# A transformer block on one core: modulation columns on the matrix engine, four load buffers, and another rank for row products

## The chip, the cores and the metric

The kernel runs on one core of one Trainium2 chip. The core has a matrix engine (TensorE, PE in the profile, with PEld for its weight loads), VectorE (DVE), ScalarE (ACT), GpSimd (POOL) and SyncE (SP), which here only issues loads. Matmuls write to PSUM, everything else lies in SBUF, and DMA engines move data between the chip's memory (HBM) and SBUF. Each engine works through its own queue in order and waits on semaphores for the others.

The metric is the device time of one execution in microseconds (us).

## The reference

The block has 256 tokens of width 2048, all in float32. What matters here is its beginning: a conditioning vector c gives a modulation vector of 12288 numbers, and its first third shifts and scales the normed input, which then meets the wide projection.

```
mod = jnp.einsum('bd,de->be', jax.nn.silu(c), w_ada[l]) + b_ada[l]
sh1, sc1, gt1, sh2, sc2, gt2 = jnp.split(mod[:, None, :], 6, axis=-1)
h = rms_norm(x, norm1_g[l]) * (1.0 + sc1) + sh1
proj = jnp.einsum('btd,dc->btc', h, w_in[l])
...
x = x + gt1 * (mixed @ w_out[l])
h = rms_norm(x, norm2_g[l]) * (1.0 + sc2) + sh2
x = x + gt2 * (jnp.square(jax.nn.relu(h @ w_up[l])) @ w_down[l])
```

`w_ada` is 2048 x 12288 and `w_in` 2048 x 10064. Between the projection and `w_out` lie a recurrent part and an attention part, which the change doesn't touch.

## The kernel before

**Layout and split matmuls.** Activations lie transposed: features on the 128 partitions in 16 chunks, tokens along the rows. A float32 product is built from three faster products: each operand is split into a rounded high part and the rest (`hhi` and `hlo` for the input, `whi` and `wlo` for weights). `split` (L190) does this for weights: ScalarE casts the loaded piece `wr` to `whi` (L193), VectorE subtracts to get `wlo` (L90).

**Modulation columns.** The number of a column of 128 modulation values is e: e = j is the shift of chunk j, e = 16 + j its scale. `ada_long(e)` (L165) loads 128 rows of the transposed `w_ada` (2048 long, 1 MB) into a slot of the tiles `ap0` and `ap1`, and `ada_dot` (L156) lets VectorE multiply them with a row `sb`, which holds silu(c) times two on every partition, and sum along the row: one *row product* gives one column of `modc`. Four slots are used for the first four loads, then two in turn (L167). A load waits until the product that read its slot is done.

**Rounds.** The projection's sum over the 16 chunks is cut into rounds: chunks 0-1, 2-3, 4-7, 8-11, 12-15 (L182). A round begins with `modulate` (L326), for each chunk: VectorE scales the normed input (`hf`), ScalarE adds the shift and rounds it (`hhi`), VectorE forms `hlo`. Its factor `am` (L387) is taken for all chunks of a round at once, so it needs all scale columns of the round. Then nine groups of output columns follow (L394): for each pair of chunks a weight piece is loaded (`weights`, L221, four buffers `wr`), split, and used in 24 matmuls (18 in the first group, which is narrower). Seven groups are evicted after each round: copied by ScalarE in the first, added to their tile by VectorE (L361) in later ones. The two groups `pvp` stay in four PSUM banks through all rounds.

The columns that a round needs are loaded in the round before: `next_ada` (L236) is called after each weight piece and takes e from the list `later` at the rate `pace`. The four columns for the first round are loaded at the start.

**Order.** The program is written with priorities: `START` comes before `STREAM` (weight loads, splits, evictions and row products), and this before `MAIN` (matmuls and the rest). A planner works out a timeline from its own estimates, takes for each engine what is ready with the best priority, and so fixes each engine's order at build time. `tc.issue_after(i)` makes an instruction come after i; `hold` and `ahold` are lists from which row products and splits take such a predecessor. After the rounds, other projections and later modulation columns are mixed into the recurrent and attention parts.

**PSUM.** Tiles named with `PX` take four banks in turn; among them are `pss` (sums of squares for the first norm) and the four `pvp`.

Of the kernel before, what the change touches and what calls it, by code (L numbers as in the profile page):

```python
# [17 lines left out]
T = 256  # L18
# [5 lines left out]


P_BADA, P_N1, P_N2, P_MU, P_A0, P_KK, P_KA, P_RK, P_LNW, P_LNB = 0, 96, 112, 128, 155, 163, 171, 179, 187, 195
P_QG, P_KG0, P_KG1, P_KG2, P_PEK, P_PEV, NPRM = 203, 204, 205, 206, 207, 223, 239

C_ID, C_MSK, C_HS, C_ONE, C_BLK, C_CUM, C_SEL, NCST = 0, 128, 192, 224, 225, 353, 609, 737

# [2 lines left out]
def block_kernel(ctx, tc, a):  # L33
# [58 lines left out]
    def stt(out, x, s, y, op0, op1):  # L92
        return V.scalar_tensor_tensor(out, x, s, y, op0=op0, op1=op1).ins  # L93
# [12 lines left out]
    STREAM = 0  # L106
    MAIN = 1 << 20
    START = -(1 << 20)


    tc.cur_priority = START
# [44 lines left out]
    def ada_dot(r, s, start, out):  # L156
        with behind():
            V.tensor_tensor_reduce(out=r, in0=r, in1=s, scale=0.5, scalar=start,  # L158
                                    op0=OP.mult, op1=OP.add, accum_out=out)

    apb = [B16("ap0", [128, 2, D]), B16("ap1", [128, 2, D])]
    apn = [0]
    SLOTS = 2

    def ada_long(e):  # L165

        n = apn[0] if apn[0] < 4 else apn[0] % SLOTS  # L167
        r = apb[n // 2][:, n % 2]
        apn[0] += 1
        nc.sync.dma_start(r, a["w_ada_t"][e * 128:(e + 1) * 128])  # L170
        ada_dot(r, sb, prm[:, P_BADA + e:P_BADA + e + 1], modc[:, e:e + 1])

    def ada(e):

# [5 lines left out]
                    modc[:, e:e + 1] if h else part)  # L180

    rounds = [(0, 2), (2, 2), (4, 4), (8, 4), (12, 4)]  # L182
    for j in range(rounds[0][1]):
        ada_long(j)
        ada_long(16 + j)


    ahold = []
# [54 lines left out]
    def proj(segs_of, W, ms, rhi, rlo, kps, evac, banks=None, first=True, last=True):  # L243


        nb = (len(ms) + 1) // 2
        ps = banks or [PM("pp") for _ in range(nb)]
        for i, kp in enumerate(kps):
            hi, lo = weights(segs_of(kp), W)
            next_ada(ada_long if starting[0] else ada)  # L250
            todo = [[(k, m) for m in range(len(ms))] for k in range(2)]
            if 0 and i == len(kps) - 1 and nb == 2:
                todo = [[(k, m) for k in range(2) for m in range(len(ms)) if m // 2 == b] for b in range(2)]
            for part in todo:
                for k, m in part:
                    (c0, cw), kc = ms[m], 2 * kp + k
                    o = ps[m // 2][0:cw, (m % 2) * 256:(m % 2) * 256 + 256]
                    mm3(o, hi[:, k, c0:c0 + cw], lo[:, k, c0:c0 + cw], rhi[:, kc], rlo[:, kc],
                        first and i == 0 and k == 0 and m % 2 == 0, last and i == len(kps) - 1 and k == 1)
                yield  # L260
        if evac:
            with prio(STREAM):
                for b in range(nb):
                    evac(b, ps[b])
# [24 lines left out]
        act(sq, xn[:, 2 * i:2 * i + 2], AF.Square)  # L289
        tt(sqs, sqs, sq, OP.add)  # L290
    for k in range(2):
        mm(pss, ones, sqs[:, k], k == 0, k == 1)

    def log_exp(behind):

# [5 lines left out]
    def rsqrt(out, x, scale, ep, tmp):  # L301

        e0 = {0.0: 0, 1e-6: 1, 64e-5: 2}[ep]
        act(out, x, AF.Ln, scale=scale, bias=eps[0:x.shape[0], e0:e0 + 1])
        i = act(out, out, AF.Exp, scale=-0.5)
        tt(tmp, out, out, OP.mult)
        stt(tmp, x, ep / scale, tmp, OP.add, OP.mult)
        stt(tmp, tmp, -0.5 * scale, out, OP.mult, OP.mult)
        stt(out, out, 1.5, tmp, OP.mult, OP.add)
        return i  # L310

    rs = T2("rs", [128, T])
    with tc.issue_after(log_exp([lastt])):
        rsqrt(rs, pss, 1.0 / D, 1e-6, T2("rst", [128, T]))

    hhi = B16("hhi", [128, KC, T], FR)
    hlo = B16("hlo", [128, KC, T], FR)
# [30 lines left out]
    pq = B8("pq", [128, 8, T])  # L348
    spq = dr.tile([128, 8, T], FT, name="spq")
    pl = cst.tile([128, 3, T], FT, name="pl")  # L350
    pvp = [PX("pvp") for _ in range(4)]
    M4 = [(i * 128, 128) for i in range(4)]

    def acc_evac(dst, first, last):
# [15 lines left out]
        groups.append(([(i * 512, 512)], 512, M4,  # L370
                       lambda b, i=i: (prk[:, i // 2, (i % 2) * 4 + 2 * b:(i % 2) * 4 + 2 * b + 2], 128, None), None))
    for i in range(2):
        groups.append(([(2048 + i * 512, 512)], 512, M4, None, pvp[2 * i:2 * i + 2]))
    for i in range(2):
        groups.append(([(i * 512, 512)], 512, M4,
                       lambda b, i=i: (prk[:, i // 2, (i % 2) * 4 + 2 * b:(i % 2) * 4 + 2 * b + 2], 128, None), None))
# [7 lines left out]
    for r, (j0, n) in enumerate(rounds):  # L384
        first, last = r == 0, r == len(rounds) - 1
        with prio(START + (1 << 18)):
            stt(am[:, j0:j0 + n], modc[:, 16 + j0:16 + j0 + n], 1.0, prm[:, P_N1 + j0:P_N1 + j0 + n], OP.add, OP.mult)  # L387
            lasth = modulate(j0, n, xn)
            if first:
                hold.extend([lasth] * 0 + [None])  # L390
        if not last:
            later.extend(e for j in range(j0 + n, sum(rounds[r + 1])) for e in (j, 16 + j))
            pace[:] = [len(later) / (len(groups) * n // 2 - 1), 0]
        for cols, W, ms, dst, banks in groups:  # L394
            g = proj(wseg(cols), W, ms, hhi, hlo, range(j0 // 2, (j0 + n) // 2),
                     dst and acc_evac(dst, first, last), banks, first or banks is None, last or banks is None)
            if last and dst and cols[0][0] >= 3360 and W == 512:
                queue.append(g)
            else:
                run(g)  # L400
        assert not later
# [731 lines left out]
            lastss[0] = mm(ps[:, 0:T], ones, x[:, i], k == 0 and i == 0, k == 1 and i == 1)  # L1133
    rs2 = T2("rs2", [128, T])
    with tc.issue_after(le):
        i = rsqrt(rs2, ps[:, 0:T], 1.0 / D, 1e-6, T2("rst2", [128, T]))
    ahold[:0] = [i, i]
    for q, t in ((0, 0), (0, 1), (1, 0)):
        tokens(q, t)
# [113 lines left out]
def _pack(inp):  # L1253

    g = {k: v[0] if k != "rel_bias" else v for k, v in inp.items()}
    p = np.zeros((128, NPRM), np.float32)

    def cols(at, v):
        v = v.reshape(-1, 128)
        p[:, at:at + v.shape[0]] = v.T  # L1260

    cols(P_BADA, g["b_ada"])
    cols(P_N1, g["norm1_g"])
    cols(P_N2, g["norm2_g"])
    cols(P_MU, g["rwkv_mu"][:3328])
    p[64:96, P_MU + 26] = g["rwkv_mu"][3328:]
    for at, k in ((P_A0, "rwkv_a0"), (P_KK, "rwkv_k_k"), (P_KA, "rwkv_k_a"), (P_LNW, "rwkv_ln_w"), (P_LNB, "rwkv_ln_b")):
        cols(at, g[k])
    cols(P_RK, g["rwkv_r_k"].reshape(-1))
    for at, v in ((P_QG, g["q_norm_g"]), (P_KG0, g["k_norm_g"][0]), (P_KG1, g["k_norm_g"][1]), (P_KG2, g["k_norm_g"][2])):  # L1270
        p[:, at] = np.concatenate([v, v])
    for at, k in ((P_PEK, "cmp_pe_k"), (P_PEV, "cmp_pe_v")):
        p[:, at:at + 16] = g[k].reshape(16, 2, 64).transpose(1, 2, 0).reshape(128, 16)
    c, onehot = _consts()
    out = {
        "xT": g["x"].T, "c": g["c"], "w_ada_t": g["w_ada"].T, "w_in": g["w_in"], "params": p, "consts": c,
        "onehot": onehot, "w2a": np.concatenate([g["rwkv_w2"], g["rwkv_w0"][None]]), "a2": g["rwkv_a2"],
        "g2": g["rwkv_g2"], "w1k": g["cmp_w1_k"], "w2k": g["cmp_w2_k"], "w1v": g["cmp_w1_v"], "w2v": g["cmp_w2_v"],
        "rel_bias": g["rel_bias"], "w_o_rwkv": g["w_o_rwkv"], "w_o_nsa": g["w_o_nsa"], "w_out": g["w_out"],
        "w_up": g["w_up"], "w_down": g["w_down"],  # L1280
    }
    return {k: np.ascontiguousarray(v) for k, v in out.items()}
# [17 lines left out]
```

## Time and profile before

| | us |
|---|---|
| median of 3 runs | 1642.96 |
| runs | 1642.14 to 1643.19 |
| the profiled execution | 1648.3 |
| its span, first to last instruction | 1646.5 |
| first matmul of round 0 starts | 27.89 |
| last row product of the rounds starts | 176.0 |

All later views are of the profiled execution, and times in them count from the start of its span. In a row of the timeline stand start, duration, engine, line, operation, output <- inputs with shapes, and in brackets how long the engine was idle before it and for whom it waited. In a row of groups the count is followed by busy us in total, mean ns of one, and the idle time before them. Helpers share lines: all matmuls are L99, most VectorE operations L90 and L93, so the names of the tiles tell them apart. In a row of waits stand who waited, for whom, the us in total, the number of waits and the longest. A few per cent of the matmul records are missing from the trace.

### The profile page before, as it was taken

How to read it: one execution, taken by the hardware profiler on the slowest of the kernel's cores; microseconds unless marked ns; L12 is line 12 of the kernel's file. 1: busy time of each engine (PE TensorE's matmuls, PEld its weight loads, DVE VectorE, ACT ScalarE, POOL GpSimd, SP SyncE). 2: the span in 40 equal slices, each digit the busy share in tenths (PEclk: the TensorE clock that was granted, in tenths of full speed). 3: DMA queues.
4: the chain of work that ended last, by engine and by line, in shares of the span. 5: the costliest groups of instructions: out<-in, count | busy, mean ns of one | idle time of the engine just before them, and what ended most of it. 6: DMA issues, size and time to landing. Idle time of an engine off the chain costs nothing.

```text
span 1646.5 us, 28130 instructions
## 1 busy us (share of the span) xinstructions
PE 1564.2 (95%) x11291; PEld 1380.2 (84%) x11291; DVE 1149.4 (70%) x1695; ACT 756.3 (46%) x1112; POOL 34.9 (2%) x60
## 2 busy tenths in 40 slices
PE   5969999999999889999999899999999999999998
PEld 4968998878889879777899788888888888888886
DVE  7999876977788766777876776666655555555555
ACT  4423358526423365656534444444444544444442
POOL 0000000000000000000000000000000000000001
PEclk9989999998999999999999999999999999999999
DMA  9999767673988777655687477878776555555564
GB/s 371 319 325 342 247 183 236 215 200 120 324 245 276 251 262 258 237 180 167 212 287 269 153 242 239 264 244 260 242 217 189 204 194 193 192 192 194 194 194 148
DMA packets 171174, 381.99 MB, mean 232 GB/s; under 512 B 29249, under 2 KB 43905, under 8 KB 166690
## 3 DMA queue, kind: packets, MB, share of 16 engines
q1 hardware_dynamic: 149344, 355.79, 65.6%
q0 software_dynamic: 4176, 14.17, 2.4%
q10 hardware_dynamic: 17523, 10.24, 2.2%
q8 instruction: 88, 1.44, 0.3%
q14 instruction: 43, 0.35, 0.1%
HBM read 370.13 MB, written 10.01 MB: 231 GB/s over the span
## 4 chain that ended last, share of the span: by engine, by line
PE 48%; DMA 4%; DVE 3%; issue 1%; ACT 1%; DVEq 0%; ACTq 0%
PE pu L99 21%; PE da L99 10%; PE db L99 10%; PE pp L99 5%; DMA ar<-in_w_ada_t 2%; DMA wr<-in_w_out 1%; DVE wlo L90 1%; PE po L99 1%; PE sps L99 1%; DMA gate<-sma 0%; ACT whi L193 0%; PE ptp L1012 0%; DVE ar L158 0%; DVE o L90 0%; ACT p L87 0%
## 5 line engine op out<-in xcount | busy, mean ns | idle before, releaser
L193 ACT CAST whi<-wr 128x1024 fp32r<-128x1024 f32 (+1 forms) x352 | 367.0, 1043 | 513.4 <-PE pp L99 125.6
L90 DVE TENSOR_TENSOR wlo<-wr,whi 128x1024 fp32r<-128x1024 f32 (+1 forms) x352 | 425.8, 1213 | 171.8 <-ACT whi L193 168.7
L99 PE MATMUL pp<-hhi,whi 128*128 128x256 f32 (+1 forms) x1072 | 309.9, 293 | 25.1 <-ACT hhi L87 22.5
L99 PE MATMUL pp<-hlo,whi 128*128 128x256 f32 (+1 forms) x1072 | 307.4, 289 | 0.2 <-DVE hlo L93 0.2
L99 PE MATMUL pp<-hhi,wlo 128*128 128x256 f32 (+1 forms) x1072 | 301.2, 290 | 6.6 <-DVE wlo L90 6.6
L90 DVE TENSOR_TENSOR wdl<-wd,wdh 128x1024 fp32r<-128x1024 f32 x128 | 156.6, 1225 | 170.9 <-ACT wdh L193 170.9
L99 PEld LDWEIGHTS pp<-hhi,whi 128*128 128x128 f32 (+1 forms) x1072 | 209.9, 197 | 33.8 <-ACT hhi L87 23.4
L193 ACT CAST wdh<-wd 128x1024 fp32r<-128x1024 f32 x128 | 134.9, 1055 | 193.7 <-PE db L99 188.6
L99 PEld LDWEIGHTS pp<-hhi,wlo 128*128 128x128 f32 (+1 forms) x1072 | 205.5, 196 | 13.0 <-DVE wlo L90 8.5
L99 PEld LDWEIGHTS pp<-hlo,whi 128*128 128x128 f32 (+1 forms) x1072 | 210.5, 196 | 5.0 <-issue 3.7
L99 PE MATMUL pu<-h2a,whi 128*128 128x512 f32 x512 | 177.2, 398 | 3.1 <-DVE h2a L93 3.1
L99 PE MATMUL pu<-h2b,whi 128*128 128x512 f32 x512 | 179.1, 397 | 0.8 <-DVE h2b L93 0.8
L99 PE MATMUL pu<-h2b,wlo 128*128 128x256 f32 x512 | 140.9, 280 | 0.0
L99 PE MATMUL pu<-h2a,wlo 128*128 128x256 f32 x512 | 135.9, 281 | 0.0
L158 DVE CUSTOM_DVE_ANT_0 ar<-ar,sb,prm 128x1024 f32<-128x1024 f32 x64 | 82.1, 1282 | 73.0 <-DMA ar<-in_w_ada_t 72.9
L99 PEld LDWEIGHTS pu<-h2b,whi 128*128 128x128 f32 x512 | 95.8, 188 | 23.9 <-DVE h2b L93 1.2
L99 PEld LDWEIGHTS pu<-h2a,whi 128*128 128x128 f32 x512 | 95.2, 189 | 24.4 <-DVE h2a L93 3.4
L99 PEld LDWEIGHTS pu<-h2a,wlo 128*128 128x128 f32 x512 | 95.5, 190 | 2.2
L158 DVE CUSTOM_DVE_ANT_0 ar<-ar,sb,adap 128x1024 f32<-128x1024 f32 x64 | 82.0, 1281 | 21.2 <-DMA ar<-in_w_ada_t 20.9
L99 PEld LDWEIGHTS pu<-h2b,wlo 128*128 128x128 f32 x512 | 95.9, 189 | 0.5
L99 PE MATMUL db<-wdh,ul 128*128 128x512 f32 x256 | 79.6, 389 | 0.0
L99 PE MATMUL db<-wdl,uh 128*128 128x512 f32 x256 | 79.6, 389 | 0.0
(342 smaller groups left out, 2676.6 us busy)
## 6 DMA issues: line engine op xcount, KB each, us to landing
wr<-in_w_in SPq DMA_DIRECT2D x136, 512.0 KB, 5.1
ar<-in_w_ada_t SPq DMA_DIRECT2D x128, 512.0 KB, 4.8
wr<-in_w_up SPq DMA_DIRECT2D x128, 512.0 KB, 4.3
wd<-in_w_down SPq DMA_DIRECT2D x128, 512.0 KB, 4.3
ap<-in_w_ada_t SPq DMA_DIRECT2D x32, 1024.0 KB, 6.6
wr<-in_w_out SPq DMA_DIRECT2D x32, 512.0 KB, 5.4
wr<-in_w_in SPq DMA_DIRECT2D x40, 256.0 KB, 3.4
wr<-in_w_o_rwkv SPq DMA_DIRECT2D x16, 512.0 KB, 4.9
```

Source lines behind the costliest of these rows:

```text
L90: return V.tensor_tensor(out, x, y, op=op).ins
L99: return PE.matmul(out, l, r, start=start, stop=stop, skip_group_check=True).ins
L158: V.tensor_tensor_reduce(out=r, in0=r, in1=s, scale=0.5, scalar=start, op0=OP.mult, op1=OP.add, accum_out=out)
L193: S.copy(hi, raw)
```

## The change

Six things change in the first rounds.

1. The columns of chunks 0 to 3 (e = 0-3 and 16-19) are no longer row products. `ada_pair` makes four columns at a time on TensorE: for j = 0 (e = 0, 1, 16, 17) and j = 2. The host lays out `w_ada` a second time for them (`w_ada_p`), in 1 MB pieces of 128 x 2048; `scz` holds silu(c) times two by chunk in the first of 32 columns and zeros in the others. Each of four loads gives four matmuls into the four 32-row strips of one PSUM bank, with the load as moving operand. ScalarE copies the bank, four matmuls with a column of ones sum the strips, and VectorE adds the bias.
2. The load slots are four throughout, not two after the first four.
3. In round 0 the list `later` holds the four loads of pair j = 2 and the columns 4, 20 and 5 of the third round, at a rate of 0.9 per weight piece; round 1 loads the remaining five at 5/8.
4. Row products get the priority `DOTS`, after `STREAM` and before `MAIN`.
5. In round 0 the `pvp` groups come last, since the two pairs use the same four PSUM banks before them.
6. In the start, the first three casts come after the first norm's exponential, the first `wlo` after the norm's last operation and the next two after the round's modulation.

```diff
+    DOTS = 1 << 19
...
-    SLOTS = 2
...
-        n = apn[0] if apn[0] < 4 else apn[0] % SLOTS
+        n = apn[0] % 4
         r = apb[n // 2][:, n % 2]
         apn[0] += 1
         nc.sync.dma_start(r, a["w_ada_t"][e * 128:(e + 1) * 128])
-        ada_dot(r, sb, prm[:, P_BADA + e:P_BADA + e + 1], modc[:, e:e + 1])
+        with prio(DOTS):
+            ada_dot(r, sb, prm[:, P_BADA + e:P_BADA + e + 1], modc[:, e:e + 1])
...
-    for j in range(rounds[0][1]):
-        ada_long(j)
-        ada_long(16 + j)
+    scz = T2("scz", [128, 16, 32])
+    V.memset(scz, 0.0)
+    sct = T2("sct", [128, 16])
+    act(sct, prm[:, P_C:P_C + 16], AF.Tanh, scale=0.5)
+    stt(scz[:, :, 0], sct, 1.0, prm[:, P_C:P_C + 16], OP.add, OP.mult)
+    adp = [None]
+
+    def ada_pair(x, after=None, copy_after=None):
+        j, q = x
+        n = apn[0] % 4
+        r = apb[n // 2][:, n % 2]
+        apn[0] += 1
+        nc.sync.dma_start(r, a["w_ada_p"][j * 256 + q * 128:j * 256 + q * 128 + 128])
+        if q == 0:
+            adp[0] = PX("adp")
+        with tc.issue_after(after) if after else contextlib.nullcontext():
+            for i in range(4):
+                mm(adp[0][32 * i:32 * i + 32], scz[:, 4 * q + i], r[:, i * 512:i * 512 + 512], q == 0, q == 3)
+        if q == 3:
+            row, ps = T2("adr", [128, 512]), PX("adc")
+            with tc.issue_after(copy_after) if copy_after else contextlib.nullcontext():
+                S.copy(row, adp[0])
+            for i in range(4):
+                mm(ps[:, i:i + 1], row[:, i * 128:i * 128 + 128], one, i == 0, i == 3)
+            for i, e in enumerate((j, 16 + j)):
+                stt(modc[:, e:e + 2], ps[:, 2 * i:2 * i + 2], 0.5, prm[:, P_BADA + e:P_BADA + e + 2], OP.mult, OP.add)
+
+    for q in range(2):
+        ada_pair((0, q))
...
-            next_ada(ada_long if starting[0] else ada)
+            next_ada((ada_pair if later and isinstance(later[0], tuple) else ada_long) if starting[0] else ada)
...
-        rsqrt(rs, pss, 1.0 / D, 1e-6, T2("rst", [128, T]))
+        firsts = rsqrt(rs, pss, 1.0 / D, 1e-6, T2("rst", [128, T]))
+    ahold.extend([firsts[0]] * 3)
+    for q in range(2, 4):
+        ada_pair((0, q), i, firsts[0])
...
-                hold.extend([lasth] * 0 + [None])
+                hold.extend([lasth, lasth, firsts[1]])
...
+        if first:
+            later[:] = [(2, q) for q in range(4)] + [4, 20, 5]
+            pace[:] = [0.9, 0]
+        elif r == 1:
+            later[:] = [e for e in later if e not in (4, 20, 5)]
+            pace[:] = [len(later) / 8, 0]
+
-        for cols, W, ms, dst, banks in groups:
+        for cols, W, ms, dst, banks in sorted(groups, key=lambda g: g[3] is None) if first else groups:
+            if banks is not None:
+                if first:
+                    pvp.extend(PX("pvp") for _ in range(2))
+                banks = pvp[2 * banks:2 * banks + 2]
```

In the start, the last two loads' matmuls of the first pair come after the sums of squares, and ScalarE's copy after the norm's exponential. `rsqrt` returns its exponential and its last operation.

More of the change, by code (lines that the diff above doesn't have):

```diff
@@ L26 @@
 P_BADA, P_N1, P_N2, P_MU, P_A0, P_KK, P_KA, P_RK, P_LNW, P_LNB = 0, 96, 112, 128, 155, 163, 171, 179, 187, 195
-P_QG, P_KG0, P_KG1, P_KG2, P_PEK, P_PEV, NPRM = 203, 204, 205, 206, 207, 223, 239
+P_QG, P_KG0, P_KG1, P_KG2, P_PEK, P_PEV, P_C, NPRM = 203, 204, 205, 206, 207, 223, 239, 255
 C_ID, C_MSK, C_HS, C_ONE, C_BLK, C_CUM, C_SEL, NCST = 0, 128, 192, 224, 225, 353, 609, 737
@@ L291, in block_kernel @@
     for k in range(2):
-        mm(pss, ones, sqs[:, k], k == 0, k == 1)
+        i = PE.matmul(pss, ones, sqs[:, k], start=k == 0, stop=k == 1, skip_group_check=True).ins
     def log_exp(behind):
@@ L308, in rsqrt @@
         stt(tmp, tmp, -0.5 * scale, out, OP.mult, OP.mult)
-        stt(out, out, 1.5, tmp, OP.mult, OP.add)
-        return i
+        return i, stt(out, out, 1.5, tmp, OP.mult, OP.add)
     rs = T2("rs", [128, T])
     with tc.issue_after(log_exp([lastt])):
-        rsqrt(rs, pss, 1.0 / D, 1e-6, T2("rst", [128, T]))
+        firsts = rsqrt(rs, pss, 1.0 / D, 1e-6, T2("rst", [128, T]))
+    ahold.extend([firsts[0]] * 3)
+    for q in range(2, 4):
+        ada_pair((0, q), i, firsts[0])
     hhi = B16("hhi", [128, KC, T], FR)
@@ L350, in block_kernel @@
     pl = cst.tile([128, 3, T], FT, name="pl")
-    pvp = [PX("pvp") for _ in range(4)]
+    pvp = []
     M4 = [(i * 128, 128) for i in range(4)]
@@ L372, in block_kernel @@
     for i in range(2):
-        groups.append(([(2048 + i * 512, 512)], 512, M4, None, pvp[2 * i:2 * i + 2]))
+        groups.append(([(2048 + i * 512, 512)], 512, M4, None, i))
     for i in range(2):
@@ L1135, in block_kernel @@
     with tc.issue_after(le):
-        i = rsqrt(rs2, ps[:, 0:T], 1.0 / D, 1e-6, T2("rst2", [128, T]))
+        i = rsqrt(rs2, ps[:, 0:T], 1.0 / D, 1e-6, T2("rst2", [128, T]))[0]
     ahold[:0] = [i, i]
@@ L1266, in _pack @@
     p[64:96, P_MU + 26] = g["rwkv_mu"][3328:]
+    cols(P_C, g["c"])
     for at, k in ((P_A0, "rwkv_a0"), (P_KK, "rwkv_k_k"), (P_KA, "rwkv_k_a"), (P_LNW, "rwkv_ln_w"), (P_LNB, "rwkv_ln_b")):
@@ L1275, in _pack @@
     out = {
-        "xT": g["x"].T, "c": g["c"], "w_ada_t": g["w_ada"].T, "w_in": g["w_in"], "params": p, "consts": c,
+        "xT": g["x"].T, "c": g["c"], "w_ada_t": g["w_ada"].T,
+        "w_ada_p": np.concatenate([np.concatenate([g["w_ada"][:, e:e + 256] for e in (j * 128, D + j * 128)], 1)
+                                   .reshape(4, 4, 128, 512).transpose(0, 2, 1, 3).reshape(512, D) for j in (0, 2)]),
+        "w_in": g["w_in"], "params": p, "consts": c,
         "onehot": onehot, "w2a": np.concatenate([g["rwkv_w2"], g["rwkv_w0"][None]]), "a2": g["rwkv_a2"],
```

## The prediction

> **What bounds the kernel now.** I read the page's first two parts first: one core, and the matrix engine (PE) is nearly always busy.
>
> ```profile
> PE 1564.2 (95%) x11291; PEld 1380.2 (84%) x11291; DVE 1149.4 (70%) x1695; ACT 756.3 (46%) x1112; POOL 34.9 (2%) x60
> ...
> PE   5969999999999889999999899999999999999998
> ...
> DVE  7999876977788766777876776666655555555555
> ...
> PEclk9989999998999999999999999999999999999999
> DMA  9999767673988777655687477878776555555564
> ```
>
> A slice is 41 us. PE's gaps are 1646.5 - 1564.2 = 82 us in all; slices 0 and 2 hold the widest, and there VectorE (DVE) and the DMA engines are at 9 of 10. The change is in that stretch, so the views by stretches of time come next (busy us of PE, PEld, DVE, ACT, POOL, then granted PE clock, DMA share, GB/s), and who waited for whom up to 200 us.
>
> ```profile
> 0.00:28.00 28.00, 9.35 (x13) 3.77 (x13) 21.98 (x40) 14.05 (x22) 0.20 (x4) 1.00 0.96 369
> 28.00:80.90 52.90, 51.98 (x413) 51.37 (x414) 47.25 (x53) 24.50 (x34) 0.00 (x0) 1.00 0.96 336
> 80.90:95.40 14.50, 1.15 (x11) 0.94 (x9) 12.82 (x17) 1.80 (x4) 0.00 (x0) 0.72 0.92 316
> 95.40:100.80 5.40, 5.40 (x24) 5.29 (x25) 4.42 (x8) 1.12 (x3) 0.00 (x0) 0.50 0.64 246
> 100.80:152.00 51.20, 48.66 (x401) 48.04 (x400) 49.45 (x56) 19.23 (x22) 0.00 (x0) 1.00 0.96 343
> 152.00:165.00 13.00, 10.80 (x78) 10.54 (x77) 12.75 (x15) 4.00 (x4) 0.00 (x0) 0.87 0.96 335
> 165.00:200.00 35.00, 35.00 (x294) 35.00 (x293) 30.12 (x37) 14.08 (x16) 0.00 (x0) 1.00 0.77 256
> ```
>
> ```profile
> PE pp L99 <- ACT hhi L87: 22.5, 2, 13.4
> ACT hhi L87 <- DVE hf L93: 14.4, 2, 11.8
> DVE ap L158 <- DMA ap<-in_w_ada_t: 4.6, 5, 1.5
> PE pp L99 <- DVE wlo L90: 4.5, 4, 2.2
> PE pvp L99 <- ACT whi L193: 1.0, 1, 1.0
> SPq L170 <- DVE modc L158: 57.2, 24, 5.3
> ```
>
> PE runs rounds 0 and 1 from 28 to 80.9, then stands 13.4 us for round 2's modulated input (hhi, behind VectorE's hf), and restarts at half clock until 100.8. After that it loses only 4.5 + 1.0 us to late weight splits, all rounds together. From 165 on it never stops. VectorE's order shows what hf was behind:
>
> ```profile
> 58.09 2.35 DVE L158 CUSTOM_DVE_ANT_0 ap<-ap,sb,prm 128x2048 f32<-128x2048 f32 x1
> ...
> 88.00 2.35 DVE L158 CUSTOM_DVE_ANT_0 ap<-ap,sb,prm 128x2048 f32<-128x2048 f32 x1 [0.28 <-DMA ap<-in_w_ada_t]
> ...
> 91.70 2.35 DVE L158 CUSTOM_DVE_ANT_0 ap<-ap,sb,prm 128x2048 f32<-128x2048 f32 x1 [1.33 <-DMA ap<-in_w_ada_t]
> ...
> 94.29 1.67 DVE L93 SCALAR_TENSOR_TENSOR hf<-xn,am,rs 128x256 f32<-128x256 f32 x4
> ```
>
> From 58 on seven row products (58.09 the first, 91.70 the last) stand before hf, two of them waiting for a load that SP could issue only when an older product had freed its slot. The bound to 95 us is VectorE's queue, with loads kept shallow by it.
>
> **The change, part by part.**
>
> *Products off VectorE.* Unit prices:
>
> ```profile
> L158 DVE CUSTOM_DVE_ANT_0 ap<-ap,sb,prm 128x2048 f32<-128x2048 f32 x32 | 74.9, 2345 | 4.6 <-DMA ap<-in_w_ada_t 4.6
> L90 DVE TENSOR_TENSOR wlo<-wr,whi 128x1024 fp32r<-128x1024 f32 (+1 forms) x54 | 63.0, 1180 | 9.2 <-ACT whi L193 9.2
> L90 DVE TENSOR_TENSOR prk<-prk,pp 128x512 f32<-128x512 f32 x24 | 15.6, 678 | 0.0
> L93 DVE SCALAR_TENSOR_TENSOR hf<-xn,am,rs 128x256 f32<-128x256 f32 x16 | 6.8, 478 | 0.1
> ```
>
> Eight of 32 products leave: 8 x 2.34 = 18.7 us of VectorE. Before, 4 of them lay in the start, 4 in round 0; 8 lay in round 1. Now three of round 1's are loaded in round 0, so five are left. Of the seven after 58 us two go for certain, 4.7 us, with the two waits of 0.28 + 1.33; if a third finds room in round 0, 7.0. So hf moves from 94.29 to between 85.7 and 88.0. Against it PE's round 0 is longer (below), which holds back VectorE's evictions in round 1 by up to 3.6 us, partly filled with products: I take hf at 86.9, and with the 1.1 us from hf to PE as before, PE restarts at 88.0 (85 to 91): **-7.4 us**.
>
> *The same sums on PE.* A pair is 16 matmuls of 128x32 weights by 128x512, four to a load in four column strips, then a copy on ScalarE, four matmuls of one column and two tiny VectorE instructions. The nearest rows are head sums in 32-column strips, one and two strips between ordinary matmuls:
>
> ```profile
> 285.21 0.28 PE L99 MATMUL pp<-hhi,wlo 128*128 128x256 f32 x1
> 285.42 1.04 PE L99 MATMUL kss<-ksq,cs 128*32 128x512 f32 x2
> 286.40 0.38 PE L99 MATMUL pp<-hhi,whi 128*128 128x256 f32 x1
> ...
> 287.81 0.28 PE L99 MATMUL pp<-hhi,wlo 128*128 128x256 f32 x1
> 288.02 1.05 PE L99 MATMUL kss<-ksq,cs 128*32 128x512 f32 x4
> 289.01 0.38 PE L99 MATMUL pp<-hhi,whi 128*128 128x256 f32 x1
> ```
>
> ```profile
> L99 PE MATMUL scp<-kcb,qn 128*128 128x32 f32 x32 | 3.7, 273 | 0.0
> ```
>
> Each fp32 matmul has two records. Two strips (x4) cost PE 289.01 - 287.81 - 0.12 = 1.08 us, no more than one strip (x2), 286.40 - 285.21 - 0.12 = 1.07: strips run together. I take 1.08 for four strips too; the other end is four in a row, 4.2. Round 0 pays four bursts (the first pair falls into the start, where PE is idle) and 8 column records at 3.7/32 = 0.12: 4 x 1.08 + 0.9 = 5.3 us (to 17.7). This speaks against the change: the Trainium skill, TensorEngine Tiling (Array Packing), Key Properties, says that changing the tiling mode drains the array, and each burst changes it twice. It has no figure for it. Here the 1.08 us contain both changes, so the sum by the row stands.
>
> These matmuls add a wait at PE's head: they wait for their load, and all projections queue behind them. Their loads come ahead of the weights of later groups, so a late one would hold PE up anyway.
>
> *The start.*
>
> ```profile
> 21.20 0.78 ACT L193 CAST whi<-wr 128x704 fp32r<-128x704 f32 x1 [1.44 <-DMA wr<-in_w_in]
> ...
> 25.28 0.15 DVE L93 SCALAR_TENSOR_TENSOR am<-modc,prm 128x2 f32<-128x2 f32 x1
> ...
> 25.69 1.21 DVE L90 TENSOR_TENSOR wlo<-wr,whi 128x1024 fp32r<-128x1024 f32 x1
> ...
> 27.89 1.22 PE L99 MATMUL pp<-hhi,whi 128*128 128x256 f32 x4 [9.15 <-ACT hhi L87]
> ```
>
> The four loads precede the weights that arrived at 21.2. From there: burst 1.1 to 2.1 (half clock), copy 0.6, column sums 0.9 to 1.8, small VectorE work 0.3: am at 24.1 to 26.0, where it was at 25.28. The split at 25.69 now waits for the modulation, so 2.6 us from am to PE become 1.4: PE at 25.5 to 27.4, say 26.2 instead of 27.89. PE then reaches the end of round 1 at 26.2 + (80.9 - 27.9) + 5.3 = 84.5, less 0.8 (the late split of round 1): 83.7. That is ahead of VectorE's 88.0, so neither the 1.7 us won at the start nor the 5.3 us of bursts enters the sum: the wait of 4.3 us covers them. Without that cover the bursts cost up to 5.3.
>
> *Half clock.* The 5.4 us to 100.8 did 24 matmul records, where 294 in 35.0 us is full rate: 2.5 us lost. A wait of 4.3 us may or may not bring it; I take half, **-1.3** (0 to -2.5).
>
> *Rank and four buffers.* Waits for splits after 95 us are 1.0 + 3.7 (4.5 less 0.8), and the stretch from 152 to 165 has 78 records where full rate gives 109: 3.7 us lost, 2.2 idle and 1.5 in clock. Together 6.2. With products last, splits come in time; but the products pile up before round 3's hf, since VectorE was 97% busy from 100.8 to 152. I put 3.0 us back there: **-3.2** (-6.2 to +4). Round 4's modulation has room: PE runs without a gap after 165 while VectorE already has pauses. Four slots change no work; they let SP, which waited 57.2 us on products, issue earlier.
>
> *The rest.* From 165 on PE is busy without a gap, so what follows moves forward as a block: 0, with 3 either way for an order of later work that comes out differently.
>
> Sum: -7.4 - 1.3 - 3.2 = -11.9. The profiled execution took 1648.3 us (span 1646.5, 1.8 around it): 1636.4. It stood 5.3 above the median of the runs, 1642.96; on that scale **1631.1 us**.
>
> **Rivals.**
>
> 1. *Loads are the bound.* Loads moved so:
>
> ```profile
> 10.00:40.00 30.00, 14.13 (x86) 12.82 (x86) 25.83 (x33) 13.58 (x22) 0.00 (x0) 1.00 1.02 406
> 40.00:100.00 60.00, 45.89 (x362) 45.26 (x361) 55.73 (x66) 21.77 (x30) 0.00 (x0) 0.89 0.92 317
> ```
>
> Round 2 needs, by sizes in the code, 16 rows of 1.05 MB, 18 weight loads (9.1 MB), x (2.1) and prefetches, 30 MB; 15 are in by 40 us (28 x 0.369 + 12 x 0.406). At 317 GB/s the rest lands at 87, then 2.3 for the product and 1.4 to PE: 91.0, so -4.4 for -7.4, in all -8.9, 1634.1. At 406 it lands at 77 and binds nothing. For the bound: a DMA share of 0.92. Against: SP's waits on VectorE lie in that very stretch. The Trainium skill, DMA: Bandwidth & Descriptors, Specifications, has about 358 GB/s for HBM per core, by which they would land at 82; the 406 of this trace is above it.
>
> 2. *Strips do not overlap, or PE waits for these loads:* round 0 pays 17.7, PE ends round 1 at 26.2 + 53.0 + 17.7 - 0.8 = 96.1 with no wait left: +0.7 - 2.5 - 3.2 = -5.0, 1638.0. The two-strip row speaks against it.
>
> 3. *No queue is late:* PE goes from round 1 into 2 at 83.7 without a wait, and the splits' 6.2 go: -11.7 - 2.5 - 6.2 = -20.4, 1622.6. It needs 4.3 us of VectorE that I don't find.
>
> 4. *Slower: products ranked last starve the modulation.* In rounds 1, 2 and 3 the last four products (9.4 us) and hf run after PE has emptied the round, and their slots hold SP's queue. Each boundary then costs 9.4 + 1.1 and the restart's 2.5: 13.0, three of them 39, against 14.5 + 2.5 + 6.2 = 23.2 now, and 3.6 for bursts less start: +19, 1662. It turns slower once the three boundaries together cost more than 20. For it: VectorE is 97% busy there. Against: hardly any product needs to be that late, since PE's round of 50 us leaves VectorE 18 x 1.18 + 14 x 0.68 + 8 x 2.34 + 8 x 0.48 = 53 at most, and neighbours overlap.
>
> 5. *Nothing arrives:* the front is gained, and later work, ordered anew, gives it back: about 1642.
>
> **How the numbers follow.** Forecast 0.50; loads 0.12; strips 0.08; nothing late 0.08; slower 0.12; given back 0.10. 0.2% is 3.3 us, about what a measurement of this kernel can tell from no change. The first four are faster by more (0.78), the last is within (0.10), starving is slower (0.12). The range runs from rival 3 with 2 us of later order, 1620, to rival 5's edge, 1643; outside it lie starving and a little at both ends.
>
> **What would show it.** The bursts: about 1.1 us each in PE's order, four strips together. VectorE's product list: 24, not 32. PE's wait for round 2's hhi: 3 to 6 us instead of 13.4, restart near 88. Waits on wlo below 1 us between rounds. If PE stands in front of hhi at round 3 or 4 for over 5 us, the rank is wrong; if it stands in round 0 before its bursts, the loads are. If all that comes out and the end doesn't move, the later order took it.

## The result, and the profile after

The changed kernel is slower: median 1666.84 us (1662.31 to 1668.64) against 1643.08 on the same chip, ratio 1.0121 with a 95% interval of 1.0101 to 1.0142. Its profiled execution took 1662.31 us, with a span of 1660.5. The forecast was 1631.1 us.

The page of the changed kernel, the rows that answer to those of before:

```profile
PE 1581.7 (95%) x11371; PEld 1389.2 (84%) x11371; DVE 1135.5 (68%) x1685; ACT 758.5 (46%) x1115; POOL 34.9 (2%) x60
...
PE   7778999999989899999999899999999999999998
...
DVE  4999577787688766778776676667665554555545
...
PEclk9989999997999999999999999999999999999999
DMA  9997666764988878655787577877776555555554
```

The changed kernel's profiled execution is the fastest of its four and 14.0 us longer than the profiled one of before; the medians are 23.8 us apart. The 14 us lie early; where the other 10 lie is left to "What stays open". I use one marker, **E**: the start of the first instruction that reads round 4's first result (ScalarE, `shq` from `pl`; the expectations below call it the first round-4 eviction). The timeline of ScalarE, before and after:

```profile
211.39 1.44 ACT L87 ACTIVATE shq<-pl,pd 128x256 f32<-128x256 f32 x3
```

```profile
225.27 1.44 ACT L87 ACTIVATE shq<-pl,pd 128x256 f32<-128x256 f32 x3
```

E comes 13.9 us later; from E to the end of the span both take the same, 1435.1 and 1435.3 us. The view by stretches from 26 us to E (length, busy us of PE, PEld, DVE, ACT, POOL, granted clock, DMA share, GB/s), before and then after:

```profile
26.00:211.40 185.40, 164.49 (x1305) 162.69 (x1306) 166.38 (x193) 70.02 (x87) 0.00 (x0) 0.95 0.89 310
...
26.00:60.00 34.00, 31.94 (x248) 31.65 (x249) 28.35 (x31) 18.51 (x28) 0.00 (x0) 1.00 0.96 350
60.00:100.00 40.00, 25.89 (x195) 25.26 (x195) 38.13 (x48) 9.58 (x12) 0.00 (x0) 0.84 0.92 316
100.00:160.00 60.00, 55.26 (x446) 54.38 (x446) 57.45 (x65) 22.17 (x24) 0.00 (x0) 0.98 0.95 339
```

```profile
26.00:225.30 199.30, 174.10 (x1345) 167.52 (x1346) 159.13 (x186) 71.20 (x89) 0.00 (x0) 0.94 0.85 291
...
26.00:60.00 34.00, 31.70 (x234) 27.59 (x234) 20.43 (x26) 17.65 (x28) 0.00 (x0) 0.90 1.03 406
60.00:100.00 40.00, 28.45 (x197) 27.47 (x198) 39.70 (x49) 9.83 (x12) 0.00 (x0) 0.88 0.99 368
100.00:160.00 60.00, 48.65 (x372) 47.16 (x371) 59.09 (x72) 19.72 (x24) 0.00 (x0) 0.94 0.86 293
```

TensorE's idle time grew from 185.4 - 164.5 = 20.9 to 25.2 us, its busy time from 164.5 to 174.1. The second part is the bursts (below, 5.3 forecast) and about 4 us of matmuls at half clock, after stalls that are now many and short. VectorE did 7.3 us less work, but in another order: from 60 to 160 us it is 99% busy. Who waited for whom from 26 to 200 us:

```profile
PE pvp L99 <- DVE wlo L90: 10.2, 4, 5.4
PE pp L99 <- DVE wlo L90: 8.1, 4, 2.9
...
PE pp L99 <- DVE pl L90: 3.7, 1, 3.7
PE pp L99 <- ACT hhi L87: 1.8, 1, 1.8
PE pp L99 <- DVE prk L90: 1.6, 1, 1.6
```

The wait of 13.4 us for `hhi` at round 2 is gone; the 1.8 us left for `hhi` are a wait ahead of the first matmul of round 0, at 26.72. In its place stand 18.3 us for weight splits (4.5 before) and 5.3 for evictions. VectorE's timeline shows one such place, and TensorE's what it cost:

```profile
52.37 2.34 DVE L159 CUSTOM_DVE_ANT_0 ap<-ap,sb,prm 128x2048 f32<-128x2048 f32 x1
...
55.43 2.34 DVE L159 CUSTOM_DVE_ANT_0 ap<-ap,sb,prm 128x2048 f32<-128x2048 f32 x1
...
57.70 2.34 DVE L159 CUSTOM_DVE_ANT_0 ap<-ap,sb,prm 128x2048 f32<-128x2048 f32 x1
...
59.98 3.15 DVE L90 TENSOR_TENSOR wlo<-wr,whi 128x1024 fp32r<-128x1024 f32 x3
```

```profile
55.11 1.73 ACT L222 CAST whi<-wr 128x1024 fp32r<-128x1024 f32 x2
```

```profile
61.25 0.38 PE L99 MATMUL pvp<-hhi,wlo 128*128 128x256 f32 x1 [2.83 <-DVE wlo L90]
```

Two casts were done at 56.84, so two splits could have run at 57.70. The engine's fixed order has a row product there, although it ranks behind the splits. Products run early all along: the last one starts at 143.16 us, where it was 176.05, while TensorE finishes its rounds later. How early shows in ScalarE's `hhi` for round 4, before and after:

```profile
184.55 1.71 ACT L87 ACTIVATE hhi<-hf,modc 128x256 fp32r<-128x256 f32 x4
```

```profile
147.31 0.51 ACT L87 ACTIVATE hhi<-hf,modc 128x256 fp32r<-128x256 f32 x1 [5.03 <-DVE hf L93]
```

That is 26.8 us ahead of E before and 78.0 ahead of it now: VectorE made a round's input long before TensorE could use it, and TensorE waited for splits meanwhile.

### The profile page after: what moved, and what is told of

The parts are those of the page before. It is cut to its first block, busy times and chain, and to the rows that moved or that the text cites. A ratio compares the mean times of both kernels' runs of the same rounds, so it can differ in the third digit from the quotient of the medians.

```text
span 1660.5 us, 28298 instructions
## 1 busy us (share of the span) xinstructions
PE 1581.7 (95%) x11371; PEld 1389.2 (84%) x11371; DVE 1135.5 (68%) x1685; ACT 758.5 (46%) x1115; POOL 34.9 (2%) x60
## 4 chain that ended last, share of the span: by engine, by line
PE 74%; DVE 11%; DMA 10%; ACT 2%; issue 2%; ACTq 0%; DVEq 0%
PE pp L99 23%; PE pu L99 21%; PE da L99 10%; PE db L99 10%; DVE wlo L90 4%; DMA wr<-in_w_in 4%; DMA ar<-in_w_ada_t 3%; DVE ap L159 2%; PE pvp L99 2%; DMA wr<-in_w_out 2%; PE po L99 1%; ACT whi L222 1%; DVE ar L159 1%; PE sps L99 1%; PE xps L99 1%
```

## The experiments

Four theories were set up. **A**: four load slots let row loads, and with them products, run ahead. **B**: the products' new rank. **C**: the third round's loads in the first round. **D**: the sums' place on TensorE, that is the bursts among the projections. "Idle" is TensorE's idle time from 26 us to E. Each ratio is to the kernel before, run beside it. E and idle come from one profiled execution each; where the same program was profiled twice (before and run 15, the changed kernel and run 2), E came out 0.4 and 1.0 us apart, so differences of 1 to 2 us in E say little.

| run | ratio (95% interval) | E, us | idle, us |
|---|---|---|---|
| before | 1 | 211.4 | 20.9 |
| changed kernel | 1.0121 (1.0101 to 1.0142) | 225.3 | 25.2 |
| 1 two slots | 1.0141 (1.0094 to 1.0187) | 218.3 | 21.6 |
| 2 no rank | 1.0145 (1.0109 to 1.0181) | 226.3 | 24.3 |
| 3 no early third round | 1.0151 (1.0115 to 1.0186) | 227.7 | 25.4 |
| 4 loads held to the pace | 1.0083 (1.0051 to 1.0115) | 215.3 | 17.7 |
| 5 before, four slots | 1.0158 (1.0130 to 1.0186) | 226.4 | 28.9 |
| 6 pairs alone | 1.0146 (1.0111 to 1.0182) | 217.4 | 21.6 |
| 7 first pair, two slots | 1.0029 (1.0010 to 1.0048) | 209.8 | 21.1 |
| 8 first pair, loads held | 1.0091 (1.0061 to 1.0121) | 210.1 | 16.6 |
| 9 short products | 1.0064 (1.0045 to 1.0083) | 214.0 | 16.2 |
| 10 half loads | 1.0227 (1.0199 to 1.0256) | 232.1 | 30.2 |
| 11 products behind splits | 1.0045 (1.0028 to 1.0062) | 211.6 | 13.8 |
| 12 before, four slots, loads held | 1.0087 (1.0058 to 1.0115) | 213.1 | 19.2 |
| 13 first pair, products behind splits | 1.0179 (1.0154 to 1.0204) | 216.4 | 21.3 |
| 14 before, four slots, products behind splits | 1.0143 (1.0118 to 1.0167) | 216.9 | 21.5 |
| 15 before, again | 0.9995 (0.9978 to 1.0011) | 211.8 | 22.3 |
| 16 as 11, one piece of slack | 1.0029 (1.0009 to 1.0049) | 202.7 | 8.2 |
| 17 as 11, two pieces of slack | 0.9985 (0.9966 to 1.0004) | 200.2 | 7.9 |
| 18 as 14, two pieces of slack | 0.9968 (0.9952 to 0.9984) | 204.7 | 13.6 |

**1. Two slots** in the changed kernel; the same line changes in `ada_long` and `ada_pair`.

```diff
-        n = apn[0] % 4
+        n = apn[0] if apn[0] < 4 else apn[0] % 2
```

> The changed kernel, but with load slots as before: four for the first four loads, then two in turn. Theory A (with four slots the 1 MB row loads run ahead of the list's rate, fill the DMA queue before the weight pieces, and their row products take VectorE from splits and evictions): the run-ahead is limited to two loads, PE's waits for wlo between 50 and 150 us shrink from about 18 to under 6 us, 1628 to 1642 us. Theory B (the low rank of the products does the harm): nothing changes in the rank, 1655 to 1668. Theory C (three of the third round's loads in round 0 swamp the first two rounds): 1650 to 1668.

The stalls for splits go, but round 2's wait comes back. The waits, and the first stretch:

```profile
PE pp L99 <- ACT hhi L87: 13.5, 2, 11.7
...
PE pp L99 <- DVE wlo L90: 1.3, 2, 0.8
```

```profile
26.00:60.00 34.00, 33.19 (x249) 29.30 (x250) 16.67 (x22) 17.85 (x28) 0.00 (x0) 0.91 0.96 350
```

From 26 to 60 us VectorE is busy for 16.7 us, 28.4 before: the products were taken from a place where it now has nothing to do, because the next loads wait for a slot. TensorE carries the bursts there for no return. E moves 7.0 us back, the ratio doesn't. So A is part of it, and not all.

**2. No rank; 3. no early third round.** In the changed kernel, the products without `prio(DOTS)`; and the first round with the four pair loads alone, round 1 with all eight columns.

```diff
-        with prio(DOTS):
-            ada_dot(r, sb, ...)
+        ada_dot(r, sb, ...)
```

```diff
-            later[:] = [(2, q) for q in range(4)] + [4, 20, 5]
+            later[:] = [(2, q) for q in range(4)]
...
-            later[:] = [e for e in later if e not in (4, 20, 5)]
-            pace[:] = [len(later) / 8, 0]
```

> The changed kernel, but row products keep the priority of splits and evictions, as before. Theory A (four slots let loads and products run ahead): 1655 to 1670, as the slots are still four. Theory B (rank): 1628 to 1645. Theory C (early third-round loads): 1650 to 1670.

> The changed kernel, but round 0 loads only the pair of chunks 2 and 3, and all eight columns of the third round are loaded in round 1 at 8/8 per weight piece. Theory A (four slots): the loads still run ahead, only from round 1 on, 1650 to 1668. Theory B (rank): 1650 to 1668. Theory C (early third-round loads): round 0 and 1 recover, 1630 to 1645.

Neither changes E by more than 2.4 us. Without the rank the instructions of VectorE, ScalarE and TensorE stand in the same order as with it: the rank decided nothing, and that run is a repetition of the changed kernel. B and C fall.

**4. Row loads held to the pace**: each behind the weight load ahead of it in the program.

```diff
+        with tc.issue_after(lastw[0]):
+            nc.sync.dma_start(r, a["w_ada_t"][...])
```

> The changed kernel, four slots, rank and early loads kept, but each row load is ordered on the load queue after the weight piece ahead of it in the program, so that it cannot run ahead of the list's rate. Theory A (run-ahead): the last row product starts near 165 us instead of 143, 1626 to 1642 us. Theory B (rank): 1652 to 1668. Theory C: 1650 to 1668, since the three early loads keep their place.

E comes 10 us earlier than in the changed kernel, and about a third of the loss goes, less than A had forecast; the last product starts at 199.15, not near 165. Running ahead does harm; whether through the queues or through VectorE this doesn't tell.

**5. The kernel before with four slots, and nothing else; 6. the pairs alone** (two slots, no rank, no early third round).

```diff
-        n = apn[0] if apn[0] < 4 else apn[0] % SLOTS
+        n = apn[0] % 4
```

> The kernel before with four load slots in turn and nothing else. Depth theory (A: four slots let row loads and products run ahead of the weights): the last product comes well before 176 us (150 or earlier), the wait for round 2's hhi shrinks below 8 us, waits on wlo rise from 4.5 to over 10 us, and the first round-4 eviction (211.4 before) moves by 0 to +6: ratio 1.000 to 1.004. Theory D (the loss is in the sums' place on TensorE: 5.3 us of bursts in a stretch that TensorE bounds, and the stalls around them): no bursts here, so ratio 0.995 to 1.000 with the first eviction of round 4 at 205 to 211. If it shows 1.01 like the change, A alone is enough.

> The changed kernel with two slots in turn after the first four loads, without the products' rank, and without the third round's loads in the first round: what is left of the change is the modulation of rounds 0 and 1 on TensorE and the order of round 0's groups. Theory D: the loss stays, ratio 1.008 to 1.015, and the bursts' 5.3 us are found in TensorE's order of round 0. Depth theory A: with two slots the loss is gone, ratio 0.995 to 1.003, the last product near 175. A loss of 1.004 to 1.007 is half of each.

I had given four slots a third of the loss at most. They are enough for all of it: E at 226.4, with the changed kernel's stalls and no pair in sight. The waits from 26 to 200 us (the one for `hhi`, 9.2, is the start's, as long as before):

```profile
PE pp L99 <- DVE wlo L90: 13.7, 8, 2.8
PE pp L99 <- ACT hhi L87: 9.2, 1, 9.2
...
PE pvp L99 <- DVE wlo L90: 6.2, 4, 3.3
```

The pairs by themselves cost 6.0 us at E, about their bursts. The two harms don't add up: with four slots the changed kernel (225.3) is no worse than without pairs (226.4).

**7., 8. The first pair alone on TensorE**, with two slots, or with four and loads held: the lines that replace `later` and `pace` in rounds 0 and 1 are left out.

```diff
-        if first:
-            later[:] = [(2, q) for q in range(4)] + [4, 20, 5]
...
-            pace[:] = [len(later) / 8, 0]
```

> The changed kernel with the first pair alone on TensorE (its burst lies in the start, where TensorE stands): columns 2, 3, 18, 19 are loaded as rows and summed by VectorE in round 0 as before, rounds 1 to 4 at the old pace, two slots in turn after the first four loads, products ranked last. Theory D: no burst among the projections, so the loss is gone: TensorE starts 1 us earlier, ratio 0.997 to 1.002. If the order of round 0's groups, the rank or the changed start carry the loss, it stays at 1.008 or more.

> As the run with the first pair alone on TensorE, but with four slots, each row load held behind the weight load ahead of it in the program. Theory D: ratio 0.995 to 1.001, and the first round-4 eviction at 205 to 212, since neither bursts nor loads that run ahead are left. Theory A would give the same; a loss of 1.005 or more speaks against both and for the four slots' products in another place.

E comes at 209.8 and 210.1, 1.6 and 1.3 before the old place, as D has it: no cost of a burst in the start, where TensorE stands, shows at E. Both ratios miss D's range. Run 8 loses some 16 us behind E, which D doesn't explain.

**9. Short products; 10. half loads**, in the changed kernel: VectorE's work without the loads', and the reverse.

```diff
-            ada_dot(r, sb, ...)
+            ada_dot(r[:, 0:256], sb[:, 0:256], ...)
```

```diff
-        nc.sync.dma_start(r, a["w_ada_t"][e * 128:(e + 1) * 128])
+        nc.sync.dma_start(r[:, 0:1024], a["w_ada_t"][e * 128:(e + 1) * 128, 0:1024])
```

> The changed kernel with each row product of rounds 1 to 4 taken over 256 of its 2048 columns (the modulation is then not the reference's); the loads are whole. About 24 x 2.0 = 48 us of VectorE's work go, no load goes. If VectorE's time is what the stalls for splits are made of, they go, and the first round-4 eviction moves from 225 to 198 to 208: ratio 0.985 to 0.998. If the weights come late because the row loads fill the queues (404 GB/s from 28 to 81 us), the eviction stays at 215 or later, with TensorE's gaps put down to whi or to the load behind it.

> The changed kernel with each row load of rounds 1 to 4 cut to its first 1024 columns, while the product still runs over 2048 (over old data in the second half, so the modulation is not the reference's). 24 x 0.52 MB = 12.6 MB go, some 31 us of the queues at 404 GB/s; VectorE's work stays. If VectorE's time is the cause, TensorE's gaps before the first round-4 eviction stay at 20 to 30 us and the eviction at 218 to 232: ratio 1.006 to 1.018. If the queues are the cause, the eviction comes at 213 or earlier and the ratio is 1.004 or less.

With half the bytes E is later still, 232.1: the loads come sooner, the products come sooner, and VectorE never pauses. The stretch from 60 to 140 us:

```profile
60.00:140.00 80.00, 51.55 (x332) 49.76 (x331) 80.00 (x101) 20.02 (x27) 0.00 (x0) 0.79 0.65 202
```

So the queues (share 0.65) are not what holds up the front of the changed kernel. With VectorE's work gone E moves 11.3 us earlier, to 214.0 and not to the 198 to 208 that I had expected. The waits of this run:

```profile
PE pp L99 <- ACT whi L222: 7.9, 3, 3.3
...
PE pvp L99 <- ACT whi L222: 4.9, 2, 3.8
```

TensorE now waits for casts, which wait for weights behind row loads (401 GB/s from 60 to 100 us): the queues are the next bound. Both edits also change the planner's order, so their sizes are not clean prices.

**11. Products behind splits**: in the changed kernel each product is held behind VectorE's split of the last weight piece ahead of it in the program. Loads, slots and bursts stay. `lastlo[0]` is the split's subtraction.

```diff
+            with tc.issue_after(lastlo[0]) if lastlo[0] else contextlib.nullcontext():
-            ada_dot(r, sb, ...)
+                ada_dot(r, sb, ...)
```

> The changed kernel with each row product held behind VectorE's split of the last weight piece that precedes it in the program; four slots, loads and bursts as they are. If the products' place ahead of the splits is the cause, TensorE's gaps for wlo fall from 20 to below 10 us between 50 and 160 us and the first round-4 eviction comes at 211 to 218: ratio 1.003 to 1.010. If the loads' run-ahead does the harm through the queues, with the products' order only its trace, the gaps stay (for whi or wlo) and the eviction at 221 or later: ratio 1.010 to 1.016.

This is the main evidence on the front's loss: one order on one engine brings E from 225.3 to 211.6. The waits from 26 to 200 us:

```profile
PE pp L99 <- DVE hlo L93: 4.5, 1, 4.5
...
PE pp L99 <- ACT hhi L87: 3.4, 2, 1.7
...
PE pvp L99 <- DVE wlo L90: 0.5, 1, 0.5
...
PE pp L99 <- DVE wlo L90: 0.3, 1, 0.3
```

0.8 us of waits for splits are left of 18.3. New are waits as round 3 begins: 1.7 us for `hhi` (the other 1.7 is the start's), behind products that now come late, and 4.5 for `hlo`. VectorE had other work ahead of that `hlo`, two splits and a product for the round after:

```profile
144.41 2.02 DVE L90 TENSOR_TENSOR wlo<-wr,whi 128x704 fp32r<-128x704 f32 x2
146.34 2.35 DVE L159 CUSTOM_DVE_ANT_0 ap<-ap,sb,prm 128x2048 f32<-128x2048 f32 x1
...
148.62 1.67 DVE L93 SCALAR_TENSOR_TENSOR hlo<-hf,modc,hhi 128x256 fp32r<-128x256 f32 x4
```

**12. The kernel before with four slots and loads held.** The edits of 5 and 4 together.

> The kernel before with four slots in turn, each row load held behind the weight load ahead of it in the program. Four slots without the pace cost 15.0 us at the first round-4 eviction (226.4 for 211.4). If the run-ahead is all of that, it is gone here: the eviction at 206 to 213, ratio 0.997 to 1.006. If four slots harm in another way (an order of the products that the deeper store allows), the eviction stays at 218 or later, ratio 1.01 or more.

E at 213.1: ahead of E, the run-ahead is nearly all that four slots cost. The ratio, 1.0087, stays above the range: 11.9 us are lost behind E.

**13., 14. The order of 11 with the first pair alone, and without pairs.**

> The changed kernel with the first pair alone on TensorE (its burst in the start), four slots, and each row product held behind VectorE's split of the last weight piece that precedes it in the program. If what is left of the loss is the bursts among the projections (5.3 us) and VectorE can carry the four products that come back (9.4 us), the first round-4 eviction comes at 204 to 209 and the ratio is 0.994 to 1.001. If VectorE is the bound of the stretch whatever the order, the four products give the bursts back: eviction at 210 to 215, ratio 1.001 to 1.008.

> The kernel before with four slots, each row product held behind VectorE's split of the last weight piece that precedes it in the program; no pairs. Four slots alone put the first round-4 eviction at 226.4 (211.4 before). If the products' place ahead of the splits is the whole harm of four slots, it comes at 206 to 213 here and the ratio is 0.997 to 1.006; if the deeper loads harm by themselves, at 218 or later, ratio 1.01 or more.

I had expected 13 to beat 11, as it has no bursts among the projections. E is 4.8 us later, beyond both of its ranges: the four products that come back to VectorE (9.4 us) cost more than four bursts. Run 14, at 216.9, lies between its two cases: without the pairs the order takes back 9.5 of four slots' 15.0 us. With the loads ahead and this order VectorE looks like the bound, and the pairs are worth about 5 us at E (runs 11 and 14). With two slots they cost 6 (run 6).

**15. The kernel before against itself.**

> The kernel before, unchanged, against itself: what the comparison gives where nothing differs. If its interval is sound, ratio 0.998 to 1.002, and the 1.0029 of the run with the first pair alone (later order of the work as before, first round-4 eviction 1.6 us earlier) is at the edge of what differs. If it comes out at 1.003 or more, the losses after round 4 (5 to 10 us in every variant) are in part the comparison's.

The comparison gives 0.9995, and its interval includes 1: no difference shows where there is none.

**16., 17. Slack in the order of 11**: a product is held behind the split of one, or two, pieces earlier. The edit to run 11 is run 17's; run 16 has `* 2`.

```diff
-    lastlo = [None]
+    lastlo = [None] * 3
...
-            lastlo[0] = split(r, hi, lo)
+            lastlo.append(split(r, hi, lo))
+            lastlo.pop(0)
```

> As the run with each product held behind VectorE's split, but behind the split of one weight piece earlier. There TensorE still stood 9.7 us for hhi and hlo ahead of rounds 3 and 4 (141.9 to 149.2, 200.4 to 203.8), behind products that came late. If one piece of slack brings these forward without putting products ahead of splits again, the first round-4 eviction comes at 204 to 210 (211.6 with no slack) and the ratio is 0.997 to 1.003; if the products go ahead of the splits again, gaps for wlo are back, eviction at 214 or later and ratio over 1.006.

> The same with two weight pieces of slack. Between the run with no slack (eviction at 211.6, ratio 1.0045) and the changed kernel, which is unlimited slack (225.3, ratio 1.0121): if the harm grows with the slack, the eviction comes later than with one piece, at 208 to 220; if the waits for hhi and hlo are worth more, earlier, at 204 to 208.

With two pieces of slack E is at 200.2, 11.2 ahead of the kernel before. Run 17's stretches, and VectorE at the place shown above:

```profile
26.00:200.20 174.20, 166.31 (x1345) 160.20 (x1346) 156.91 (x190) 71.55 (x88) 0.00 (x0) 0.99 0.93 334
...
100.00:160.00 60.00, 58.66 (x486) 58.02 (x484) 57.27 (x67) 22.57 (x25) 0.00 (x0) 1.00 0.94 333
```

```profile
55.09 2.35 DVE L159 CUSTOM_DVE_ANT_0 ap<-ap,sb,prm 128x2048 f32<-128x2048 f32 x1
...
57.36 1.22 DVE L90 TENSOR_TENSOR wlo<-wr,whi 128x1024 fp32r<-128x1024 f32 x1
58.50 2.34 DVE L159 CUSTOM_DVE_ANT_0 ap<-ap,sb,prm 128x2048 f32<-128x2048 f32 x1
60.77 2.02 DVE L90 TENSOR_TENSOR wlo<-wr,whi 128x704 fp32r<-128x704 f32 x2
```

Products and splits alternate. E is earlier than either case of the expectation had it. TensorE's idle time falls to 7.9 us, its clock stays at 0.99. But of 11.2 us the whole time shows 0.15%, within the interval of no change: the rest is given back behind E.

**18. The same without pairs**: the kernel before, four slots, two pieces of slack.

> The kernel before with four slots, each product held behind the split of two weight pieces earlier, and no pairs: against the run with pairs and the same order (first round-4 eviction at 200.2) it tells what the modulation on TensorE is worth by itself. If VectorE bounds the stretch once the order is right, the eight products that come back to it (four of them in the start, 9.4 us from 28 us on) against bursts of 5.3 us give an eviction at 203 to 209. If the order and the four slots are all of the gain, 198 to 202. If four slots need the pairs, 213 or later as in the run without slack (216.9).

E at 204.7: of the front's gain of 11.2 us the slots with the order bring 6.7, the pairs 4.5. In whole time this run is the fastest, ratio 0.9968 (0.9952 to 0.9984), median 1643.27 against 1647.48. Whether it is faster than run 17 isn't told apart: the intervals overlap.

**What stays open.** Behind E most versions lose 5 to 25 us more than their E explains. The changed kernel's median lies 23.8 us behind, E 13.9. There the planner's order of the later work differs from before's in all versions but run 7, which still loses some 6 us. So it may not be order alone. Run 2 is the changed kernel's own program, and a stretch of the recurrent part, between the same two instructions, took before, in the changed kernel and in run 2:

```profile
368.08:494.63 126.55, 120.80 (x1538) 107.77 (x1537) 98.81 (x168) 58.92 (x88) 2.70 (x5) 0.93 0.72 231
```

```profile
381.34:504.06 122.72, 115.45 (x1473) 104.20 (x1472) 95.49 (x164) 57.47 (x85) 2.70 (x5) 0.90 0.68 225
```

```profile
382.63:511.36 128.73, 121.04 (x1473) 109.20 (x1472) 96.64 (x165) 57.46 (x85) 2.71 (x5) 0.85 0.67 220
```

The same program took 6 us more with a clock of 0.85 for 0.90. From E to the end its two profiled executions took 1435.3 and 1447.6 us, so a difference of 12 us behind E between two single profiles needs no difference in order. Over whole executions the mean granted clock is 0.974 in the changed kernel's four timed runs and 0.980 over the 97 of the kernel before that ran beside the experiments; an estimate from these: 0.6% of 1582 busy us is about 9.5 us, some 4 of them ahead of E. What brings the lower clock behind E, the order of the later work or something else, was not tried: some 10 of the 23.8 us have no shown cause.

## Why the prediction was wrong

**Products off VectorE: the relief came, the gain didn't.** 24 products are left, and the modulated input of round 2 was ready earlier than forecast: `hf` at 79.33 us, where 86.9 was forecast. TensorE doesn't wait for it at all, where it waited 13.4. But the step put TensorE's restart at 88.0 for a gain of 7.4, and by a count of its matmuls TensorE reached round 2 only at about 104 us, 95.4 before. The products ran early at the splits' expense, which the step had not priced. (Its first reading of the page is also off in one place: in slice 0 VectorE's digit is 7, not 9.)

**The same sums on PE: size right, cover wrong.** One burst in TensorE's timeline:

```profile
32.62 0.28 PE L99 MATMUL pp<-hhi,whi 128*128 128x256 f32 x1
32.83 1.06 PE L99 MATMUL adp<-ap,scz 128*32 128x512 f32 x8
33.83 0.39 PE L99 MATMUL pp<-hlo,whi 128*128 128x256 f32 x1
```

Four strips run together in 1.06 us, 1.09 from start to start by the forecast's own measure (1.08 forecast), and TensorE starts at 26.72 (26.2). But the prediction set bursts and start at nothing, covered by a wait of 4.3 us for round 2. That wait is gone, so the 5.3 us are on the path: the step itself had named this price. Run 6, with two slots again, shows 6.0 at E.

**Half clock: wrong sign.** -1.3 was forecast; about +4 came. One stall of 13.4 us and five short ones became ten of 0.5 to 5.4 us. From 26.7 us to E, 95 of the matmuls in the trace start some 0.21 us after the one ahead of them, at half rate, where 57 did before (117 and 46 in the second profile of each) and 0.12 is full rate; 38 more at 0.094 us each are 3.6 us. The clock rows alone mislead here: in the first stretch they say 0.90 for 1.00, but in both kernels round 0's first matmuls stand 0.21 us apart until about 32.4.

**Rank and four buffers: the step that failed.** The prediction put it at -3.2, with the words "With products last, splits come in time" and "Four slots change no work; they let SP [...] issue earlier". The first was taken from the rank's meaning, and run 2 shows that the rank changed no instruction's place. By its rule the planner takes what is ready in its own timeline, so a product that is ready goes ahead of a split that isn't yet, whatever its rank; that timeline itself was not looked at. The second was the costlier. Loads that come earlier make products ready earlier, and each takes 2.34 us of the engine that every split and eviction passes through. Four slots alone cost 15.0 us at E (run 5), as much as the whole loss of the front. In the changed kernel an order on the products takes 13.7 of 13.9 away (run 11); two slots take 7.0 (run 1), and what stays then is about the bursts' price, uncovered, as run 6 has it. Waits for splits and evictions rose to 23.6 us where 6.2 was to be saved.

**Rivals.** The slower one had the right sign and the right engine, and the wrong mechanism: it feared products that come too late, and they came too early. Its own mechanism shows in small in run 11, where TensorE waits 1.7 us for round 3's `hhi` behind products that came late. "Loads are the bound" is out as the cause (run 10) and in as the next bound (run 9). In the changed kernel the queues moved 406 GB/s from 26 to 60 us. The Trainium skill, DMA: Bandwidth & Descriptors, Specifications, gives about 358 GB/s as the limit per core; the 406 of this trace is above it. "Given back later" wasn't the case here, as the front gained nothing, but it is what became of run 17's gain.

**The sum.** The front's -11.9 was a possible result: run 17 has -11.2 at E, with the waits for splits at 5.1 us. The kernel as changed doesn't have the order for it. That the two numbers are close is partly luck: in run 17 the terms are not the forecast's. And the step "The rest", put at 0 with 3 either way, was too small: behind E run 17 gives back some 9.5 us, and the changed kernel loses some 10, for a reason that stays open.

## What to carry to other kernels

A deeper buffer is not free work moved earlier: it also makes the consumer's work ready earlier, and on an engine that is 97% busy that work can take the place of what the bound engine needs next. A rank in this planner breaks ties among what is ready; if two streams must alternate, say so with a dependency, and give it some slack (none cost 11 us at E against two pieces, unlimited slack 25). Work moved to another engine pays only where the engine relieved is late: ask, before counting the saving, which stretch the removed instructions stood in, and what covers the new ones if the wait that you remove was their cover.

## What the runs showed of the hardware

One program's executions differ with the clock: 97 of the kernel before lie between 1639.26 and 1656.11 us, and fall by 1.0 us for each 0.001 of mean granted clock (a line through them, correlation -0.69). Stalls of a few microseconds can cost more than their length: with idle time of 25.2 us the changed kernel had some 4 us more of half clock than before, and with 7.9 us (run 17) the clock was 0.99. It is no fixed rate: run 12 had 19.2 us idle, in stalls of up to 3.2, and a clock of 0.99. Four column strips of 128x32 weights by 128x512 cost as much as one or two strips, both changes of shape included: 1.09 us from start to start, against 1.07 and 1.08.
